# Two transformer blocks on one core: the modulation moved to TensorE's column groups, and the work around the norms reordered

## The chip, the cores and the metric

The kernel runs on one core of a Trainium2 chip. The time is that of one execution on the device in microseconds. The core's engines run in parallel and wait for each other by semaphores: TensorE (PE; its weight loads are shown apart as PEld), VectorE (DVE), ScalarE (ACT), GpSimd (POOL) and SyncE (SP). Transfers are issued from SP's and POOL's queues and carried out by 16 DMA engines.

## The reference

256 tokens of width 1024 pass through two blocks. In the first, a hybrid mixer (an mLSTM and a sliding-window attention), a cross-attention to 256 memory rows and a convolutional feed-forward net are each followed by a layer norm of the residual sum. The second block is modulated by a vector c:

```python
mod = jax.nn.silu(c) @ mod_w + mod_b            # (1, 1024) @ (1024, 6144)
shift1, scale1, gate1, shift2, scale2, gate2 = jnp.split(mod, 6)
h = rms_norm(x, g_pre_mix) * (1 + scale1) + shift1
# three branches of h (short convolution, stick-breaking attention, state space), merged with sigmoid gates
x = x + gate1 * rms_norm(merged @ w_o, g_post_mix)
h2 = rms_norm(x, g_pre_ffn) * (1 + scale2) + shift2
gt, up = jnp.split(h2 @ w_ffn_in, 2)
x = x + gate2 * rms_norm((silu(gt) * up) @ w_ffn_out, g_post_ffn)
```

All data are float32. The modulation is one vector times a matrix of 24 MB; its six vectors of 1024 are needed on all token rows.

## The kernel before

**Products.** Every float32 weight tile of 128 x 1024 is fetched into a staging tile (`wst`, four of them, from SP's queue), then split into a high and a low part of type float32r: ScalarE writes the high part (line 194), VectorE the rest (line 195). Each product is then three matmuls. Two orders are used: `mmB` (lines 369 to 373) keeps a weight tile of 128 x 128 stationary and streams 256 tokens, so that the result stands feature-major; `mmA` (lines 379 to 381) keeps 128 tokens stationary and streams up to 512 weight columns, so that it stands token-major. `weight_order` lists all weights in the order of use; `pump` splits as many of them ahead as there are homes (`WSP` = 5 pairs of tiles and, between certain points, three more by `widen`), and `done` gives a home back.

**Order of the work.** The instruction order of each engine is written out by hand: side chains are Python generators that `beside` advances by one step between matmuls, and the table `LAG` says after how many steps each goes on. `finish` ends a projection: for its last `lead` weights it does all products of token tile 0, then all of tile 1, and calls `after(tt)` as each tile's sum is complete. `boundary` builds that `after` for the four norms that stand in the way (`ln1`, `ln2`, `ln3`, and `x4`, the two norms between the mixer and the feed-forward net of the second block). It issues the norm chain of tile 0 (`layer_norm`, or `rms`, small operations on VectorE and ScalarE), then that of tile 1 interleaved with a `fill`, work for TensorE that doesn't need both tiles. `tsplit` transposes a tile's rows back to feature-major on TensorE (line 466) and splits them (lines 469 and 472).

**The feed-forward nets.** 5632 up-columns go in 11 groups `j` of 512 (256 of the gate and 256 of the value). Group 0 is done token-major by `up_first`: tile 0's part is a fill of the boundary, its result is transposed back by `turn`. The others are feature-major. The down products of earlier groups are interleaved; the last six down weights are left to `finish`.

**The modulation.** Twelve halves of 512 columns, each summed over 8 k-tiles of 128. Four halves are `raw_product`s (line 320): silu(c) of a k-tile, broadcast to 128 columns, is the stationary operand, so that the sum stands on all partitions; they are fills of the boundaries `ln2` (1), `ln3` (2) and `x4` (1), and their tiles come through the weight staging. The other eight are summed on VectorE (lines 1362 and 1364) from tiles of their own (`raw`, two buffers, SP's queue), and one matmul by ones (line 1372) brings the sum to all partitions. These steps are spread over both feed-forward nets and the branches (`mods_beside`). `mod_rows` adds the bias and multiplies the gain, which are broadcast to all partitions by transfers of 512 KB.

## Time and profile before

| | |
|---|---|
| time, median of 3 runs | 871.06 us (868.68 to 872.78) |
| the profiled execution's own time | 875.15 us |
| its span, first to last instruction | 873.4 us |
| mean granted TensorE clock | 0.987 |
| HBM read | 174.59 MB, 201 GB/s over the span |

The rows further down are of that one execution. "Busy" is the time in which an engine works on an instruction. A matmul's end is modelled, so a matmul's mean time is longer than the step to the next one; where a price per matmul is wanted, it is read from the starts. Behind "<-" stands what ended an idle time. An instruction is named by engine, line of the kernel, operation and tiles (out<-in). Float32 matmuls that are not split are issued as two instructions each.

### The profile page before, as it was taken

How to read it: one execution, taken by the hardware profiler on the slowest of the kernel's cores; microseconds unless marked ns; L12 is line 12 of the kernel's file. 1: busy time of each engine (PE TensorE's matmuls, PEld its weight loads, DVE VectorE, ACT ScalarE, POOL GpSimd, SP SyncE). 2: the span in 40 equal slices, each digit the busy share in tenths (PEclk: the TensorE clock that was granted, in tenths of full speed). 3: DMA queues.
4: the chain of work that ended last, by engine and by line, in shares of the span. 5: the costliest groups of instructions: out<-in, count | busy, mean ns of one | idle time of the engine just before them, and what ended most of it. 6: DMA issues, size and time to landing. Idle time of an engine off the chain costs nothing.

```text
span 873.4 us, 14226 instructions
## 1 busy us (share of the span) xinstructions
PE 846.1 (97%) x5580; PEld 759.5 (87%) x5580; DVE 626.6 (72%) x1047; ACT 426.2 (49%) x629; POOL 35.5 (4%) x52
## 2 busy tenths in 40 slices
PE   7999999899999999999989999999999999999996
PEld 6999878898799999999748987999995899999994
DVE  5688797665669987786777888589779765555443
ACT  5554663465256655554245645344454554444431
POOL 2000100000000000000010000002310000000000
PEclk9999999999999999999999997899999999999998
DMA  8854755285387886676186775476775686665511
GB/s 284 285 156 132 253 193 194 87 289 163 97 284 243 264 262 210 201 254 229 39 301 247 260 235 177 129 232 200 228 241 178 220 259 194 197 190 192 181 62 49
DMA packets 49860, 176.61 MB, mean 202 GB/s; under 512 B 5660, under 2 KB 5808, under 8 KB 49664
## 3 DMA queue, kind: packets, MB, share of 16 engines
q1 hardware_dynamic: 46224, 162.76, 56.9%
q0 software_dynamic: 3568, 12.92, 4.5%
q8 instruction: 44, 0.72, 0.3%
q14 instruction: 24, 0.20, 0.1%
HBM read 174.59 MB, written 1.07 MB: 201 GB/s over the span
## 4 chain that ended last, share of the span: by engine, by line
PE 74%; DMA 4%; DVE 3%; ACT 2%; issue 1%; DVEq 0%; ACTq 0%
PE pb L369 14%; PE pb L373 13%; PE pb L371 13%; PE pa L379 8%; PE pa L380 8%; PE pa L381 8%; PE pb L320 3%; DVE wl L195 2%; ACT wh L194 1%; DMA wst<-in_w_a 1%; PE pb L1372 1%; DMA wst<-in_mod_w 1%; PE pb L1172 1%; DMA wst<-in_ffn_up 1%; DMA wst<-in_xa_wq 1%
## 5 line engine op out<-in xcount | busy, mean ns | idle before, releaser
L195 DVE TENSOR_TENSOR wl<-wst,wh 128x1024 fp32r<-128x1024 f32 (+3 forms) x260 | 315.7, 1223 | 157.4 <-ACT wh L194 155.2
L194 ACT CAST wh<-wst 128x1024 fp32r<-128x1024 f32 (+3 forms) x260 | 267.5, 1036 | 274.9 <-PE pb L373 135.1
L379 PE MATMUL pa<-wh,hh 128*128 128x512 f32 x176 | 69.6, 395 | 0.0
L380 PE MATMUL pa<-wl,hh 128*128 128x512 f32 x176 | 69.2, 393 | 0.0
L381 PE MATMUL pa<-wh,hl 128*128 128x512 f32 x176 | 69.0, 392 | 0.0
L369 PE MATMUL pb<-x3h,wh 128*128 128x256 f32 x320 | 53.4, 289 | 0.0
L369 PE MATMUL pb<-x2h,wh 128*128 128x256 f32 x320 | 52.5, 286 | 0.5 <-DVE cv L626 0.5
L369 PE MATMUL pb<-x4h,wh 128*128 128x256 f32 x320 | 51.6, 283 | 0.0
L373 PE MATMUL pb<-x3l,wh 128*128 128x256 f32 x320 | 51.4, 283 | 0.0
L371 PE MATMUL pb<-x3h,wl 128*128 128x256 f32 x320 | 51.4, 283 | 0.0
L373 PE MATMUL pb<-x2l,wh 128*128 128x256 f32 x320 | 51.2, 282 | 0.0
L371 PE MATMUL pb<-x2h,wl 128*128 128x256 f32 x320 | 51.2, 282 | 0.0
L371 PE MATMUL pb<-x4h,wl 128*128 128x256 f32 x320 | 51.1, 282 | 0.0
L373 PE MATMUL pb<-x4l,wh 128*128 128x256 f32 x320 | 51.1, 282 | 0.0
L369 PEld LDWEIGHTS pb<-x2h,wh 128*128 128x128 f32 x320 | 44.4, 190 | 2.6 <-issue 1.9
L626 DVE SCALAR_TENSOR_TENSOR cv<-pb,sm,cv 128x255 f32<-128x255 f32 (+2 forms) x106 | 43.5, 473 | 3.5 <-ACT cv L622 3.5
L369 PEld LDWEIGHTS pb<-x3h,wh 128*128 128x128 f32 x320 | 44.2, 191 | 1.9 <-issue 1.6
L369 PEld LDWEIGHTS pb<-x4h,wh 128*128 128x128 f32 x320 | 44.3, 190 | 1.1 <-issue 0.5
L373 PEld LDWEIGHTS pb<-x3l,wh 128*128 128x128 f32 x320 | 44.1, 192 | 0.0
L371 PEld LDWEIGHTS pb<-x3h,wl 128*128 128x128 f32 x320 | 44.1, 191 | 0.0
L373 PEld LDWEIGHTS pb<-x2l,wh 128*128 128x128 f32 x320 | 43.9, 191 | 0.0
L371 PEld LDWEIGHTS pb<-x2h,wl 128*128 128x128 f32 x320 | 43.8, 190 | 0.0
(432 smaller groups left out, 1614.9 us busy)
## 6 DMA issues: line engine op xcount, KB each, us to landing
wst<-in_ffn_up SPq DMA_DIRECT2D x44, 512.0 KB, 4.6
wst<-in_ffn_in SPq DMA_DIRECT2D x44, 512.0 KB, 4.0
raw<-in_mod_w SPq DMA_DIRECT2D x32, 512.0 KB, 4.5
wst<-in_w_gl SPq DMA_DIRECT2D x24, 512.0 KB, 4.2
wst<-in_ffn_down SPq DMA_DIRECT2D x22, 512.0 KB, 4.2
wst<-in_ffn_out SPq DMA_DIRECT2D x22, 512.0 KB, 3.6
wst<-in_mod_w SPq DMA_DIRECT2D x16, 512.0 KB, 4.3
wst<-in_w_qk SPq DMA_DIRECT2D x12, 512.0 KB, 4.7
```

The source lines that it names most:

```text
L194: A.copy(xh, src)
L195: V.tensor_tensor(xl, src, xh.bitcast(F32), ALU.subtract)
L320: T.matmul(pm_, cs[:, k:k + 1].to_broadcast([P, P]), st[:, e, :], start=(k == 0), stop=(k == KT - 1))
L369: T.matmul(dst, wh[:, k - k0, c0:c0 + P], xh[:, k, t0:t1], start=(k == ks[0]), stop=False)
L371: T.matmul(dst, wl[:, k - k0, c0:c0 + P], xh[:, k, t0:t1], start=False, stop=False)
L373: T.matmul(dst, wh[:, k - k0, c0:c0 + P], xl[:, k, t0:t1], start=False, stop=(k == ks[-1]))
L379: T.matmul(dst[:, c0:c1], xh[:, k, tsl], wh[:, kw, c0:c1], start=first, stop=False)
L380: T.matmul(dst[:, c0:c1], xh[:, k, tsl], wl[:, kw, c0:c1], start=False, stop=False)
L381: T.matmul(dst[:, c0:c1], xl[:, k, tsl], wh[:, kw, c0:c1], start=False, stop=last)
L626: V.scalar_tensor_tensor(dst[:, j:S], ps[:, 0:S - j], taps[K - 1 - j], dst[:, j:S], ALU.mult, ALU.add)
L1172: T.matmul(pl[:, e * S:(e + 1) * S], vx[:, mt, ct * P:(ct + 1) * P], pT[:, mt, :], start=(mt == 0), stop=(mt == 1))
L1372: T.matmul(pm_, ones, acc_, start=True, stop=True)
```

## The change

- **Modulation.** All six vectors go through TensorE. For each k-tile four matmuls, each with 32 broadcast columns as the stationary operand and 256 of the 1024 columns streaming, write partitions 0 to 31, 32 to 63, 64 to 95 and 96 to 127 of one bank. Bursts of four k-tiles (12 in all) are placed in both feed-forward nets (5 and 2), in the boundary `ln3` (1) and beside the branches (4). Bias and gain are added in that layout (128 x 256, rows repeated by the host); the result goes through a small DRAM tile to all partitions. The matrix tiles of 512 KB (48) come on POOL's queue into four buffers. `raw_product`, the sums on VectorE and the matmuls by ones go.
- **Feed-forward nets.** The first two groups (`NF` = 2) are token-major. Within a k-tile pair the three kinds of matmul are grouped. Both groups of tile 0 are the fill of `ln2` and `x4`, both of tile 1 follow before the net begins.
- **Boundaries.** With `n0` = 99 tile 0's chain is issued whole; after tile 1's last product come tile 0's transposes, then the fill with a few steps of tile 1's chain before each fill step (`n4`) and `p1` splits after it; all but the last `f2` fill steps, then tile 1's transposes. `lead` is 8 for w_o (was 4), 6 for xa_wo (was 4). `ahead` allows a few splits as `finish` frees homes.
- **Homes.** `WSP` is 6; `lend` and `widen` hand out further pairs: four from the cross-attention's space for the up-columns of `ln2`, two from the tile that later holds the branches' outputs, two before `x4`. `done` splits at most two at a time.
- **Rows and tables.** Gains and biases of the norms are loaded in halves into tiles `cv0` and `cv1`, earlier than before. The attention's bias band comes ready from the host and is loaded on SP's queue, where two small matmuls, a copy and a bounce through DRAM stood. The scan's row sums are loaded by pairs of heads into two buffers instead of all at once.

The diff, cut to its core:

```diff
             for i in range(m):
+                if tt == 0:
+                    pre(items[i][2])
                 for c0, c1 in halves(ncol):
                     mmA(acc[tt], items[i][0](), 0, items[i][1], items[i][2], tt, c0, c1, first and i == 0, False)
                 if tt == 1:
                     done(go=False)
+                    freed()
                 mid()
             for c0, c1 in halves(ncol):
                 for i in range(m, n):
                     w, x, kx = items[i]
+                    if tt == 0 and c0 == 0:
+                        pre(kx)
                     mmA(acc[tt], w(), 0, x, kx, tt, c0, c1, first and i == 0, i == n - 1)
                     if tt == 1 and c1 == ncol:
                         done(go=False)
+                        freed()
                 mid()
             after(tt)
...
-    def boundary(name, chain, src, x, fill, n_fill):
+    def boundary(name, chain, src, x, fill, n_fill, before=lambda: None):
         cs_ = []
 
         def after(tt):
+            if tt == 0:
+                before()
             c = chain(tt)
             cs_.append(c)
             if tt == 0:
@@ -487,6 +480,7 @@
             c0 = cs_[0]
             while next(c0, "end") != "end":
                 drain(c, LAG[name + ".n3"])
+            pump(LAG[name + ".p0"])
             drain(fill, LAG[name + ".f0"])
             t = tsplit(src(0), x, 0)
             drain(c, LAG[name + ".n1"])
@@ -496,16 +490,26 @@
             for _ in range(n_fill - LAG[name + ".f0"] - LAG[name + ".f2"]):
                 drain(c, LAG[name + ".n4"])
                 next(fill, None)
-            n = 0
-            while next(c, "end") != "end":
-                n += 1
-                if n == LAG[name + ".p"]:
-                    pump(LAG[name + ".pn"])
+                pump(LAG[name + ".p1"])
+            drain(c)
             t = tsplit(src(1), x, 1)
             next(t)
             drain(fill)
             drain(t)
+            pump(LAG[name + ".p2"])
         return after
...
+    def ahead(name):
+        left = [LAG[name + ".t0"], LAG[name + ".t1"]]
+
+        def freed():
+            if left[0]:
+                left[0] -= 1
+            elif left[1]:
+                left[1] -= 1
+                pump(1)
+        return freed
...
     def bias():
-        pv = bankB()
-        T.matmul(pv[0:8, 0:384], rel, oh, start=True, stop=False)
-        T.matmul(pv[0:8, 0:384], ones[0:1, 0:8], mrow, start=False, stop=True)
-        band = tp.tile([8, 384], F32, tag="t", bufs=4, name="band")
-        V.tensor_copy(band, pv[0:8, 0:384])
-        d1 = dp.tile([8, 384], F32, name="d1")
-        G.dma_start(d1, band)
-        G.dma_start(kbias, bass.AP(tensor=d1.tensor, offset=d1.offset + 1, ap=[[1, P], [384, 8], [1, S]]))
+        band = a["band"]
+        nc.sync.dma_start(kbias, bass.AP(tensor=band.tensor, offset=band.offset + 1, ap=[[1, P], [384, 8], [1, S]]))
         flags.add("bias")
...
     rows = []
     wout = projA(acc, "w_out", xm, boundary("ln1", lambda tt: layer_norm(acc[tt], xs, x1, rows, tt), lambda tt: x1[:, tt, :],
-                                            xb, fill_xk(), 2 * len(fill1())), ks=(4, 5, 6, 7, 0, 1, 2, 3))
-    for k0 in (4, 6):
-        until(f"xm{k0}")
-        drain(wout, 2)
-    settle()
+                                            xb, fill_xk(), 2 * len(fill1()), before=settle), ks=(4, 5, 6, 7, 0, 1, 2, 3),
+                 lead=LAG["w_out.lead"], freed=ahead("ln1"), pre=lambda k: until(f"xm{k // 2 * 2}"))
+    until("xm4", "qk0", "qk1", "qk2", "qk3")
+    rows.extend([RowOf("ln1_g", "cv0"), RowOf("ln1_b", "cv1")])
+    drain(wout, 8 - LAG["w_out.lead"])
+    drain(wout)
...
+    def up_first(name, x, out):
+        ws, got, late_ = [], {}, []
+
+        def take(f, tt, pt):
+            got[f, tt] = tp.tile([P, 512], F32, tag="t", name=nm("up"), bufs=4)
+            out(got[f, tt], pt)
 
         def product(tt):
-            pt = bankA()
-            got.append(pt)
-            for i in range(4):
-                if tt == 0:
-                    ws.append(weights(name, i))
-                for kw in range(2):
-                    mmA(pt, ws[i], kw, x, 2 * i + kw, tt, 0, 512, i + kw == 0, i + kw == 4)
-                if tt == 1:
-                    done(go=False)
-                yield
+            while late_:
+                take(*late_.pop(0))
+            tsl = slice(tt * P, tt * P + P)
+            for f in range(NF):
+                pt = bankA()
+                for i in range(4):
+                    if tt == 0:
+                        ws.append(weights(name, 4 * f + i))
+                    (wh, wl), (xh, xl) = ws[4 * f + i], x
+                    for n, (x_, w_) in enumerate(((xh, wh), (xh, wl), (xl, wh))):
+                        for kw in range(2):
+                            T.matmul(pt, x_[:, 2 * i + kw, tsl], w_[:, kw, :], start=(i + n + kw == 0), stop=(i + n + kw == 6))
+                    if tt == 1:
+                        done(go=False)
+                    if i == 3 and tt == 0:
+                        late_.append((f, tt, pt))
+                    elif i == 3:
+                        take(f, tt, pt)
+                    yield
 
         return product, got
...
+    up1 = up_first("ffn_up0", xb, lambda st, pt: A.copy(st, pt))
+
+
+    def room2():
+        settle()
+        s_xp.close()
+        s_k8.close()
+        wider.append(widen(4, first_of["ffn_up0"] + 4 * NF, side=None))
+        pump()
...
     wo = projA(acc, "xa_wo", xo, boundary("ln2", lambda tt: layer_norm(acc[tt], x1, x2, rows, tt), lambda tt: x2[:, tt, :],
-                                          xb, raw0, 4 * len(RAW["ln2"]) - LAG["ln2.raw"] + 4), lead=LAG["wo.lead"])
-    for n in range((8 - LAG["wo.lead"]) // 2):
-        until(f"xo{n}")
-        drain(wo, 2)
-    drain(raw0, LAG["ln2.raw"])
-    settle()
+                                          xb, up1[0](0), 4 * NF, before=room2), lead=LAG["wo.lead"],
+               pre=lambda k: until(f"xo{k // 2}"), freed=ahead("ln2"))
+    until("xo0")
     drain(wo)
...
+    def act1_first(j, up0, hid, later):
         ps = [bankB(), bankB()]
-        turn(st[0], ps, 0)
-        a0, a1 = act1(0, 0, ps[0], hid), act1(0, 1, ps[1], hid)
-        later.extend([lambda: turn(st[1], ps, 1), a0[0], lambda: (a0[1](), a1[0]()), a1[1], a1[2]])
+        turn(up0[1][j, 0], ps, 0)
+        turn(up0[1][j, 1], ps, 1)
+        a0, a1 = act1(j, 0, ps[0], hid), act1(j, 1, ps[1], hid)
+        later.extend([a0[0], lambda: (a0[1](), a1[0]()), a1[1], a1[2]])
...
-    mods, rows_of = {}, {}
-
-
-    def mod_rows(half, pm_):
-        g, cs_ = half // 2, HF[half % 2]
-        if g not in mods:
+    mods = {}
+
+
+
+    raws = {}
+    n_raw = [0]
+
+    def raw_ahead():
+        if n_raw[0] < 6 * KT:
+            g, k = divmod(n_raw[0], KT)
+            raws[g, k] = fetch(mp, "raw", 4, a["mod_w"][g, k].rearrange("p (a b) -> p a b", a=4), G)
+            n_raw[0] += 1
+
+    def mod_steps():
+        for _ in range(4):
+            raw_ahead()
+        yield
+        for g in range(6):
+            bt = mp.tile([P, 2, 256], F32, tag="brow", name=nm("brow"))
+            G.dma_start(bt, a["mod_rows"][g])
+            res = mp.tile([P, 256], F32, tag="mres", name=nm("mres"), bufs=2)
+            for k0 in range(0, KT, 4):
+                pm_ = bankB()
+                for k in range(k0, k0 + 4):
+                    st = raws.pop((g, k))
+                    for j in range(4):
+                        T.matmul(pm_[32 * j:32 * j + 32, 0:256], cs[:, k:k + 1].to_broadcast([P, 32]), st[:, 256 * j:256 * j + 256],
+                                 start=(k == k0), stop=(k == k0 + 3))
+                V.tensor_tensor(res, pm_[:, 0:256], res if k0 else bt[:, 0, :], ALU.add)
+                for _ in range(4):
+                    raw_ahead()
+                if k0 + 4 < KT:
+                    yield
+            if g in (1, 4):
+                V.scalar_tensor_tensor(res, res, 1.0, bt[:, 1, :], ALU.add, ALU.mult)
+            elif g in (2, 5):
+                V.tensor_tensor(res, res, bt[:, 1, :], ALU.mult)
...
+            d = dp.tile([4, 256], F32, name=nm("d"))
+            G.dma_start(d, res[0:P:32, :])
+            G.dma_start(mods[g], d.rearrange("a b -> (a b)").unsqueeze(0).to_broadcast([P, D]))
...
-            rows3.extend([row(mp, "ln3_g"), row(mp, "ln3_b")])
+        spread(5, 2, NJ - 1, j, point)
+        if point == 1 and j == NJ - 1:
+            rows3.extend([RowOf("ln3_g", "cv0"), RowOf("ln3_b", "cv1")])
+
+            spare.extend(hilo("spare"))
+            parts_of = [tuple(t[:, 4 * i:4 * i + 4, :].rearrange("p a b -> p (a b)") for t in spare) for i in range(2)]
+            spare.append(lend(parts_of, first_of["w2_a"] + 8))
+            pump()
...
-        for h in RAW["ln3"]:
-            yield from raw_product(h)
+        mod_step()
+        yield
...
-    chains.append(mods_beside(n_steps(LAG["h.f1"], 10)))
+    chains.append(mods_beside(4))
...
-    widen(3, len(order))
+    wider.append(widen(3, len(order)))
+    wider.append(widen(2, first_of["ffn2_in0"] + 4 * NF, side=None))
+    pump()
...
-    drain(projA(acc, "w_o", xg, boundary("x4", chain4, lambda tt: hs_[tt], xb, fill4(), 4 * len(RAW["x4"]) + 4),
-                lead=LAG["w_o.lead"]))
+    def up2_out(st, pt):
+        A.activation(st[:, 0:256], pt[:, 0:256], AF.Silu)
+        V.tensor_tensor(st[:, 0:256], st[:, 0:256], pt[:, 256:512], ALU.mult)
+
+    up2 = up_first("ffn2_in0", xb, up2_out)
+
+    drain(projA(acc, "w_o", xg, boundary("x4", chain4, lambda tt: hs_[tt], xb, up2[0](0), 4 * NF),
+                lead=LAG["w_o.lead"], freed=ahead("x4")))
+    drain(up2[0](1))
+    narrow(wider.pop())
...
-        raw_rows_out()
-        spread(n_steps(10, 12), 1, NJ - 1, j, point)
+        spread(2, 3, NJ - 2, j, point)
```

## Rows read from the trace of the kernel before

**Rows 1.** The page, parts 1 and 2: busy time by engine; granted clock in 40 slices.
```profile
PE 846.1 (97%) x5580; PEld 759.5 (87%) x5580; DVE 626.6 (72%) x1047; ACT 426.2 (49%) x629; POOL 35.5 (4%) x52
...
PEclk9999999999999999999999997899999999999998
```

**Rows 2.** Stretches: length, busy us of PE, PEld, DVE, ACT, POOL, granted clock, DMA.
```profile
300.00:320.00 20.00, 20.00 (x149) 19.04 (x148) 18.27 (x28) 11.70 (x17) 0.00 (x0) 1.00 0.82 261
432.44:461.79 29.35, 24.30 (x94) 14.32 (x92) 20.61 (x45) 11.34 (x20) 2.62 (x6) 1.00 0.81 274
534.00:550.80 16.80, 15.70 (x55) 11.03 (x54) 11.26 (x23) 6.13 (x12) 0.53 (x1) 0.59 0.47 156
665.32:681.90 16.58, 14.78 (x52) 8.49 (x50) 13.22 (x38) 4.66 (x13) 0.00 (x0) 0.90 0.43 127
```

**Rows 3.** Timeline of the stick-breaking stage: start us, us, engine, line, operation, idle before.
```profile
535.24 0.70 PE L1621 MATMUL pa<-qb,kb 64*128 64x256 f32 x2 [1.10 <-DVE lk L1614]
```

**Rows 4.** Groups of instructions on PE by form: busy us, mean ns, idle before.
```profile
L320 PE MATMUL pb<-wst,cs 128*128 128x512 f32 x64 | 30.6, 623 | 1.2 <-DMA wst<-in_mod_w 1.2
...
L1372 PE MATMUL pb<-macc,triu 128*128 128x512 f32 x16 | 9.1, 650 | 0.0
```

**Rows 5.** Timeline at the second norm, PE.
```profile
231.63 3.60 PE L320 MATMUL pb<-wst,cs 128*128 128x512 f32 x8
...
235.07 1.04 PE L466 MATMUL pb<-ident,x 128*128 128x128 f32 x8
```

**Rows 6.** Groups of instructions on DVE.
```profile
L1364 DVE SCALAR_TENSOR_TENSOR macc<-raw,cs,macc 128x512 f32<-128x512 f32 x56 | 43.0, 767 | 1.1
```

**Rows 7.** Timeline of the attention's output products, PE.
```profile
518.81 0.66 PE L1640 MATMUL pb<-att,v 128*64 128x256 f32 x4
519.30 0.40 PE L1641 MATMUL pb<-att,v 128*64 128x128 f32 x4
519.62 0.74 PE L369 MATMUL pb<-x3h,wh 128*128 128x256 f32 x4
```

**Rows 8.** The same in the window 518.80 to 518.83 us.
```profile
518.81 0.44 PE L1640 MATMUL pb<-att,v 128*64 128x256 f32 x2
```

**Rows 9.** The same, weight loads.
```profile
518.81 0.20 PEld L1640 LDWEIGHTS pb<-att,v 128*64 128x64 f32 x4
```

**Rows 10.** DMA issues: queue, count, size of each, us to landing.
```profile
raw<-in_mod_w SPq DMA_DIRECT2D x32, 512.0 KB, 4.5
```

**Rows 11.** Timeline of feature-major products, PE.
```profile
568.60 0.64 PE L369 MATMUL pb<-x3h,wh 128*128 128x256 f32 x4
569.08 0.64 PE L371 MATMUL pb<-x3h,wl 128*128 128x256 f32 x4
```

**Rows 12.** Timeline of token-major products, PE.
```profile
230.47 0.40 PE L380 MATMUL pa<-wl,xoh 128*128 128x512 f32 x1
...
230.70 0.40 PE L381 MATMUL pa<-wh,xol 128*128 128x512 f32 x1
```

**Rows 13.** Timeline after the first norm, PE.
```profile
169.27 0.74 PE L369 MATMUL pa<-x1h,wh 128*128 128x256 f32 x4 [1.83 <-ACT wh L194]
```

**Rows 14.** Timeline at the second norm, tile 1's chain on DVE, first and last rows.
```profile
231.98 0.68 DVE L561 SCALAR_TENSOR_TENSOR r<-x,pa 128x512 f32<-128x512 f32 x1
...
236.99 1.41 DVE L577 SCALAR_TENSOR_TENSOR x<-x,rr,ln_b 128x512 f32<-128x512 f32 x2
```

**Rows 15.** Timeline at the third norm, tile 1's chain on DVE, first and last rows.
```profile
434.44 0.68 DVE L561 SCALAR_TENSOR_TENSOR r<-x,pa 128x512 f32<-128x512 f32 x1
...
445.77 1.42 DVE L1407 SCALAR_TENSOR_TENSOR h__760_4655<-h__760_4655,rr,mod 128x512 f32<-128x512 f32 x2
```

**Rows 16.** Timeline at the second block's boundary: tile 0's chain, and PE after it.
```profile
658.92 0.59 ACT L587 ACTIVATE junk<-pa 128x512 f32<-128x512 f32 x1
...
668.07 1.41 DVE L1407 SCALAR_TENSOR_TENSOR h__1127_7018<-h__1127_7018,rr,mod 128x512 f32<-128x512 f32 x2
668.96 1.29 PE L466 MATMUL pb<-ident,h__1127_7018 128*128 128x128 f32 x8 [1.76 <-DVE h__1127_7018 L1407]
```

## What I expect, before any run of the change

> **What bounds the kernel now.** I read the page first. TensorE is busy for 97% of the span, VectorE for 72%, and the granted clock is full in nearly every slice [rows 1]. The busy time of two mid-kernel stretches says the same: from 300 to 320 us TensorE is busy for 20.00 of 20.00 us while VectorE is busy for 18.27 [rows 2]. So in the feed-forward nets VectorE is loaded but not waited for, and work taken from it there buys nothing by itself. Work taken from TensorE counts one for one.
>
> Then I looked for time that TensorE loses, stretch by stretch [rows 2]. The hand-over to the last norm of the first block (432 to 462 us) has 24.30 busy of 29.35 us, the hand-over inside the second block (665 to 682) 14.78 of 16.58 at a granted clock of 0.90, and the stick-breaking stage (534 to 551) a granted clock of 0.59, its lower level of 1.2 GHz for most of the stretch. There the clock fell after TensorE had idled 1.10 us for VectorE amid short fp32 products [rows 3]. These places and the start and tail are the only losses worth naming, so the change can win in two ways: fewer TensorE microseconds in the modulation, or shorter waits in these stretches.
>
> **The modulation.** Before, 4 of its 12 halves are products of 8 matmuls with a broadcast stationary operand, each issued as two instructions: 64 instructions of 512 columns. The other 8 are summed on VectorE and end in one matmul by ones, 16 instructions [rows 4]. Eight of them take 235.07 - 231.63 = 3.44 us, or 0.43 each [rows 5]. TensorE spends 80 x 0.43 = 34.4 us. All of that goes, and with it 56 multiply-adds of 767 ns and 8 multiplies on VectorE [rows 6].
>
> What comes: 6 x 8 x 4 = 192 matmuls of 256 columns with 32 stationary columns, 384 instructions. By the 0.43 us per 512 columns each costs 0.215 us alone. The question is whether four column groups run at once. The trace has no such case with four, but one with two: the attention output writes partitions 0 to 63 and 64 to 127 of one bank in turn. Four instructions of 256 columns (two passes in each of two groups) take 519.30 - 518.81 = 0.49 us, where one after another would be 0.86 [rows 7]. Within the first 0.02 us both groups have started [rows 8]. So two run side by side. From line 1640's first start to the next full-width product it is 519.62 - 518.81 = 0.81 us, of which 2 x 0.215 + 2 x 0.107 = 0.64 are passes; some 0.2 us goes to changing over. Hence a burst of 4 k-tiles is 8 x 0.215 + 0.2 = 1.92 us if four groups overlap, and 12 bursts are 23.0 us. The bounds: overlap only in twos, 12 x (16 x 0.215 + 0.2) = 43.7 us; none at all, 12 x (32 x 0.215 + 0.2) = 85.0 us. I take the full overlap, since the nearest row shows each further group for nothing. Modulation: **-11.4 us** (+9.3 and +50.6 at the bounds).
>
> The four weight loads of line 1640 lie within 0.20 us, at a time when its first matmuls (0.44 us) are still running, on the same rows [rows 8, 9]. The Trainium skill, "TensorE: Matmul & The Clock Gate", section "Part 3: Packing small matmuls — row/col tiling", says that a weight load overlaps a running matmul only when its row group differs. All column groups here share all rows, so by it each of the 96 passes would show its four loads, at 0.20 us for four [rows 9] some 19 us more, and the gain would be gone. This trace disagrees, so the sum doesn't use it.
>
> **Moved transfers.** The 48 loads of the modulation (512 KB; the 32 in their own buffers land 4.5 us after issue) [rows 10] go from SP's queue to POOL's, four buffers instead of two. On SP they waited for VectorE's sums in front of the weights; on POOL they wait for a burst that TensorE has just been given. Behind them on POOL stand the small bounce, the broadcast rows, the scan's row loads and the additions into the merged tile. I cost this at nothing: POOL is busy for 35.5 us of the span [rows 1], so its queue has room, and the first five bursts spread over much of the 195 us between the second and third norm [rows 14, 15]. In the mix stage, where bursts lie closer, 2 MB per step and 0.5 MB per weight can compete; the staged and split weights cover that, and if they don't it is part of the stall case below.
>
> **Token-major columns.** One more block of 512 up-columns in each net changes from 96 matmuls of 256 columns (0.48 / 4 = 0.12 us each, 11.5 us) [rows 11] to 48 of 512 (0.23 each, 11.0 us) [rows 12]: -1.0 us for two nets. It adds 12 transposes of 1.04 / 8 = 0.13 us [rows 5], +1.6. Sum **+0.6 us**; its worth is that it fills a boundary.
>
> **Norm boundaries.** Each now runs tile 0's chain in one piece under tile 1's products, then tile 0's transposes, then a fill that needs only tile 0, while tile 1's chain runs.
> - First norm: TensorE waited 1.83 us for weight splits after the fill [rows 13]; one split per fill step now comes under it. A layer-norm chain lasts 231.98 to 236.99 + 1.41, 6.4 us [rows 14], against 5.6 us of tile-1 products (24 x 0.23), so some 0.8 us shows instead. -1.0 us.
> - Second norm: the raw product hid everything. Now the first copy shows between transposes and products, +0.5 us; the 8 token-major steps (48 x 0.23 = 11.0 us) cover the 6.4 us chain.
> - Third norm: tile 1's chain with the modulation took 434.44 to 445.77 + 1.42 = 12.75 us [rows 15]. The stretch of 29.35 us holds 28 raw instructions (12.0 us), so without a change in waiting it would become 29.35 - 12.0 + one burst of 1.9 = 19.3 us. I expect tile 0's chain 2.3 us late, 12.75 for tile 1, 1.3 to its first product, 16.4 us; up to four weight splits of 1.22 lie between, 21.3 us. The middle is no change: 0 (-3 to +2).
> - Second block: 8 instead of 4 of the w_o weights now come per token tile, so tile 1's products cover the chain of 658.92 to 668.07 + 1.41 = 10.6 us, and the wait of 1.76 us goes [rows 16]. But three of the eight weights of the fill are not yet split and queue behind tile 1's chain on VectorE. 0 (-2 to +2).
>
> **Stick-breaking stage.** VectorE loses half of the multiply-adds here, so the idle 1.10 us may go [rows 3], and with it the clock's fall, which costs 16.8 x 0.41 = 6.9 us [rows 2]. I take -2.0, between 0 and -8. The bias table from the host saves two small products in the start, which waits for loads there: 0 (to -1).
>
> **Sum.** -11.4 + 0.6 - 1.0 + 0.5 + 0 + 0 - 2.0 + 0 = -13.3 us. The profiled execution took 875.15 us, of which 873.4 are the span, so it would become 861.9. It lies 4.1 us over the median of the runs; on the median, 871.06 - 13.3 = 857.8. **Forecast 858 us.**
>
> **Rivals.**
> - *Slower: the groups overlap only in twos.* One mechanism, in the bursts: 43.7 instead of 23.0 us gives 858 + 20.7 = 879 us. It decides from an overlap of about 2.2, where 12 x (32 x 0.215 / 2.2 + 0.2) is near the 34.4 that go. For it: no row has more than two. Against: the second group cost nothing. The written order speaks for something like it too: each group's two passes are written one after the other, so if starts keep the written order, each group trails by a pass, 48 x 4 x 0.215 = 41.3 us, 876 us; but in [rows 7] the second group's line 1640 runs before the first group's line 1641, against the written order. The Trainium skill, same page and section, states that matmuls start and end strictly in order; the trace disagrees unless the build reorders, which it can't show. Chance of either 0.13.
> - *Boundary stalls.* The fills are shorter without raw products; if TensorE idles 4 us at the third norm or in the second block, the clock may fall as in [rows 2], 6.9 us for one such fall, or late weights cost as much: 865, 872 for two. For it: the 1.76 us wait was followed by a clock of 0.90. Against: the first norm's 1.83 us was not [rows 1]. Chance 0.15.
> - *The stick stage keeps its clock.* 6 us more than I took: 852. Chance 0.12.
> - My forecast, 858 (851 to 864 with the bounds of the small terms): 0.60.
>
> **Range and chances.** Something like 0.5% is what these runs can tell from no change, 866.7 to 875.4. Faster: 0.60 + 0.12 + half the stalls, 0.78. Slower: most of the first rival, 0.12. Same: 0.10. The range is 847 to 870, which leaves out the first rival and part of the double stall.
>
> **What would show it.** Right: the bursts start four matmuls within some 0.05 us and last near 1.9 us; no multiply-adds on raw tiles; TensorE's waits in the four hand-overs add to no more than now; full clock after the third norm. Wrong: bursts of 3.6 us or more, the clock at half after a hand-over, TensorE waiting for weight splits in the second block, or for loads in the mix stage.

## The result, and the profile after

| | median of runs | ratio to the kernel before | 95% interval |
|---|---|---|---|
| before | 870.41 us (868.68 to 872.78) | | |
| changed | 883.12 us (878.94 to 884.25) | 1.010 | 1.0056 to 1.0145 |
| forecast | 858 us (847 to 870) | | |

The quotient of the two medians is 1.015, at the upper end of the interval. So the change made the kernel some 1% slower (0.6 to 1.5%); I had given that 0.12. The profiled execution took 883.34 us (span 881.2), where the sum said 861.9: 21 us are to be found.

They are not in the modulation. From the page of the changed kernel (engines, clock in 40 slices, then the group of the burst products):

```profile
PE 842.3 (96%) x5796; PEld 756.9 (86%) x5796; DVE 576.1 (65%) x979; ACT 425.2 (48%) x632; POOL 64.5 (7%) x112
PEclk9999999999999999999979998899999999999999
...
L1355 PE MATMUL pb<-raw,cs 128*32 128x256 f32 x384 | 23.2, 382 | 0.0
```

And the first burst in the timeline, cut to its first 0.03 us and then whole:

```profile
295.70 0.42 PE L1355 MATMUL pb<-raw,cs 128*32 128x256 f32 x4
...
295.70 1.93 PE L1355 MATMUL pb<-raw,cs 128*32 128x256 f32 x32
297.57 0.38 PE L354 MATMUL pb<-x2h,wh 128*128 128x256 f32 x1
```

Four instructions start within 0.03 us, and 32 take 297.57 - 295.70 = 1.87 us, little more than eight passes of 0.215 us: the four column groups run side by side. All 384 are busy for 23.2 us, where I had 23.0. VectorE fell from 72% [rows 1] to 65%. Yet TensorE is busy for 842.3 us, hardly less than the 846.1 of before [rows 1], and the clock has three slices below full in mid-kernel. TensorE stands idle for 38.9 us of the span, where it was 27.3. So it waits more. Windows of the changed kernel (length, TensorE busy, granted clock, DMA share, GB/s): xa_wo; from there to the first net's loop; the hand-over at the third norm; the stick-breaking stage; w_o and the hand-over in the second block:

```profile
201.71:231.20 29.49, 27.60 (x121) 1.00 0.32 108
231.20:260.29 29.09, 26.00 (x131) 1.00 0.41 139
418.64:469.36 50.72, 42.88 (x219) 0.90 0.58 195
543.78:557.43 13.65, 12.34 (x46) 0.50 0.29 84
647.33:705.06 57.73, 50.81 (x218) 0.97 0.42 133
```

The same stretches of the kernel before, without the stick-breaking stage:

```profile
204.90:231.41 26.51, 26.51 (x122) 1.00 0.34 106
231.41:251.58 20.17, 20.17 (x86) 1.00 0.67 209
413.86:470.62 56.76, 51.71 (x220) 1.00 0.53 180
643.24:689.03 45.79, 43.99 (x180) 0.96 0.58 192
```

Each of these four stretches now leaves 1.9 to 7.8 us idle, 19.7 us in all, where before it was 6.9. At the third norm the clock goes to its lower level behind the waits, which costs up to 50.72 x 0.10 = 5.1 us. The stick-breaking stage runs at 1.2 GHz for 13.65 us, no less than before [rows 2]. What TensorE waited for (us, times, longest), in the first two windows, at the third norm, and in the second block:

```profile
PE pb L354 <- DVE cv L641: 2.8, 1, 2.8
PE pa L364 <- ACT xoh L1181: 1.9, 2, 1.2
PE pa L1220 <- ACT x2h L460: 0.2, 1, 0.2
...
PE pa L366 <- DVE x3l L463: 3.5, 1, 3.5
PE pb L457 <- DVE h__742_4702 L1403: 3.4, 1, 3.4
...
PE pa L1220 <- ACT wh L194: 2.9, 2, 1.7
PE pa L1220 <- DVE wl L195: 2.7, 3, 1.4
PE pa L1220 <- DVE x4l L463: 0.9, 1, 0.9
```

Most of this, 13.3 of 18.3 us, ends on VectorE (DVE), the rest on ScalarE, at moments when TensorE has nothing else to do. The wait of 3.5 us shows it best (timeline; a bracket is the idle time before an instruction, and what ended it):

```profile
438.66 1.84 DVE L195 TENSOR_TENSOR wl<-wst,wh 128x776 fp32r<-128x776 f32 x2
440.25 0.40 PE L365 MATMUL pa<-wl,x3h 128*128 128x512 f32 x1
440.42 0.42 DVE L1357 TENSOR_TENSOR mres<-pb,mres 128x256 f32<-128x256 f32 x1
440.87 0.42 DVE L1365 TENSOR_TENSOR mres<-mres,brow 128x256 f32<-128x256 f32 x1
441.21 0.68 DVE L576 SCALAR_TENSOR_TENSOR r<-x,pa 128x512 f32<-128x512 f32 x1
443.46 0.68 DVE L463 TENSOR_TENSOR x3l<-pb,x3h 128x512 fp32r<-128x512 f32 x1
444.20 0.50 PE L366 MATMUL pa<-wh,x3l 128*128 128x512 f32 x1 [3.55 <-DVE x3l L463]
```

The low half of tile 0 (x3l) stands in VectorE's queue behind two weight splits, the modulation's own two steps and the first steps of tile 1's chain. TensorE has transposed tile 0 and started on it, and can only wait. In the kernel before, raw products of 0.43 us each [rows 5] lay in this place.

The theory to test: **a microsecond of TensorE is worth one only where TensorE is the last to be ready.** The raw products taken away stood in hand-overs, where TensorE waits for VectorE anyway; 11 of the 12 bursts stand in loops, where it does not. Rivals: the new order of the hand-overs loses by itself (rival 1), or the moved loads do (rival 2).

### The profile page after: what moved, and what is told of

Its sections match the earlier page's. It is cut to its first block, busy times and chain, and to the rows that moved or that the text cites. A ratio compares the mean times of both kernels' runs of the same rounds, so it can differ in the third digit from the quotient of the medians.

```text
span 881.2 us, 14633 instructions
## 1 busy us (share of the span) xinstructions
PE 842.3 (96%) x5796; PEld 756.9 (86%) x5796; DVE 576.1 (65%) x979; ACT 425.2 (48%) x632; POOL 64.5 (7%) x112
## 3 DMA queue, kind: packets, MB, share of 16 engines
HBM read 174.02 MB, written 1.09 MB: 199 GB/s over the span
## 4 chain that ended last, share of the span: by engine, by line
PE 73%; DVE 7%; ACT 2%; issue 2%; DMA 1%; POOL 0%; DVEq 0%; ACTq 0%
PE pb L354 13%; PE pb L356 13%; PE pb L358 13%; PE pa L364 6%; PE pa L366 6%; PE pa L365 6%; PE pa L1220 4%; PE pb L1355 2%; DVE wl L195 2%; ACT wh L194 1%; PE pa L358 1%; PE pa L356 1%; PE pa L354 1%; PE pb L1178 1%; PE pb L1152 1%
## 5 line engine op out<-in xcount | busy, mean ns | idle before, releaser
L201 POOL DMA_DIRECT2D raw<-in_mod_w x48 | 25.2, 530 | 389.4 <-PE pb L1355 301.3
L354 PE MATMUL pb<-x2h,wh 128*128 128x256 f32 x288 | 47.2, 287 | 2.8 <-DVE cv L641 2.8
L356 PE MATMUL pb<-x2h,wl 128*128 128x256 f32 x288 | 46.5, 284 | 0.0
L358 PE MATMUL pb<-x2l,wh 128*128 128x256 f32 x288 | 46.3, 283 | 0.0
L354 PE MATMUL pb<-x4h,wh 128*128 128x256 f32 x288 | 46.2, 283 | 0.0
L358 PE MATMUL pb<-x4l,wh 128*128 128x256 f32 x288 | 46.0, 282 | 0.0
L356 PE MATMUL pb<-x4h,wl 128*128 128x256 f32 x288 | 46.0, 282 | 0.0
L354 PEld LDWEIGHTS pb<-x2h,wh 128*128 128x128 f32 x288 | 40.2, 193 | 5.5 <-issue 4.3
L354 PEld LDWEIGHTS pb<-x4h,wh 128*128 128x128 f32 x288 | 39.8, 190 | 1.3 <-issue 0.4
L356 PEld LDWEIGHTS pb<-x2h,wl 128*128 128x128 f32 x288 | 39.9, 193 | 0.0
```

The lines of the kernel that those rows point to most:

```text
L201: (queue or nc.sync).dma_start(st[:, :n].rearrange("p (a b) -> p a b", a=src.shape[1]), src)
L354: T.matmul(dst, wh[:, k - k0, c0:c0 + P], xh[:, k, t0:t1], start=(k == ks[0]), stop=False)
L356: T.matmul(dst, wl[:, k - k0, c0:c0 + P], xh[:, k, t0:t1], start=False, stop=False)
L358: T.matmul(dst, wh[:, k - k0, c0:c0 + P], xl[:, k, t0:t1], start=False, stop=(k == ks[-1]))
```

## The experiments

For the comparisons below the span is cut into stages by TensorE's own products: the first one that reads xo, the last of xa_wo, the last up-product of the first net, the first unit of the mix, the first of w_o, and the last of all. Lengths in us, one profiled execution each:

| kernel | start, first norm | xa_wo | second norm, first net | third norm | mix | second block, second net | tail | span |
|---|---|---|---|---|---|---|---|---|
| before | 204.9 | 26.5 | 182.5 | 56.8 | 172.6 | 221.7 | 8.5 | 873.4 |
| before, no modulation | 205.1 | 26.5 | 181.9 | 50.8 | 167.3 | 221.0 | 8.4 | 861.1 |
| before with bursts | 210.2 | 26.5 | 192.2 | 52.9 | 175.5 | 223.0 | 8.4 | 888.7 |
| changed | 201.7 | 29.5 | 187.4 | 50.7 | 178.0 | 225.5 | 8.4 | 881.2 |
| changed, no modulation | 203.1 | 29.5 | 177.2 | 49.3 | 167.4 | 220.9 | 8.4 | 855.8 |
| four vectors on VectorE, mended | 200.4 | 27.7 | 179.8 | 48.1 | 172.8 | 221.0 | 8.7 | 858.6 |

The first stage differs by 5 us between profiles of kernels whose start is the same (205 and 210 in those made from before), so the other stages tell more than the span. The mix has a spread of its own: how long the lower clock lasts in its stick-breaking stage differs from trace to trace, from nothing to 17.07 us, and up to half of that time is lost.

**1 and 2. Both kernels without modulation.** The loads, products and sums go, the rows are the biases. In the kernel before, the empty steps stay in the hand-overs.

```diff
-            use(("raw", 4 * half + i), product)
-            raw_used.add(("raw", 4 * half + i))
             yield
-        raw_rows.append((half, pm_))
+        raw_rows.append((half, None))
...
-        V.tensor_tensor(res[:, cs_], pm_, mb[:, cs_], ALU.add)
+        V.tensor_copy(res[:, cs_], mb[:, cs_])
```

> The kernel before with the modulation's loads, products and sums left out (the modulation rows are the bias rows alone). 34.4 us of TensorE work go. Theory (lost cover): the 28 raw products at the three hand-overs were what hid the norm chains, so the hand-overs open and the time falls by only about 17 us, to 853, with the clock at half after the third norm or in the second block. Rival 1 (the new order of the hand-overs loses by itself): nothing opens here, the time falls by nearly all of it, to about 837. Rival 2 (transfers): the 24 MB of loads count too, 837 or less.

Measured: 866.35 us, ratio 0.9932 (0.9898 to 0.9966). 34.4 us of TensorE work left, and the time fell by 0.7%, about 6 us: less than even the theory expected. Windows of the second norm, third norm and second block, and the waits in them:

```profile
231.56:253.62 22.06, 16.56 (x70) 0.85 0.18 62
413.47:464.28 50.81, 41.37 (x188) 0.87 0.39 129
631.61:677.53 45.92, 38.76 (x164) 0.93 0.45 151
```

```profile
PE pa L370 <- ACT x2h L460: 2.8, 1, 2.8
PE pa L372 <- DVE x2l L463: 2.7, 1, 2.7
...
PE pa L370 <- ACT x3h L460: 3.1, 2, 2.9
PE pa L371 <- DVE wl L195: 3.0, 1, 3.0
...
PE pb L457 <- DVE h__1068_6830 L1387: 4.1, 1, 4.1
```

The hand-overs open: where the raw product hid the second norm, 5.5 us are idle (0 before) and the clock falls; at the third norm 9.4 us are idle (5.1 before); in the second block 7.2 (1.8 before). The first window shows how the saving is lost. The raw product of 6.9 us is gone from it, and it is 1.9 us longer than before: 5.5 us of idle time and 22.06 x 0.15 = 3.3 us by the lower clock make up the 8.8. By stages, 9.5 us of products left the first net's stage and 0.6 came off it; 13.8 left the third norm's and 5.9 came off; 7.7 left the second block's and 0.7 came off.

In the changed kernel:

```diff
-            raws[g, k] = fetch(mp, "raw", 4, a["mod_w"][g, k].rearrange("p (a b) -> p a b", a=4), G)
...
-                V.tensor_tensor(res, pm_[:, 0:256], res if k0 else bt[:, 0, :], ALU.add)
+                if k0 == 0:
+                    V.tensor_copy(res, bt[:, 0, :])
```

> The changed kernel with the modulation's loads and products left out (rows are the bias rows alone). 23 us of bursts go. Theory: the bursts cost what they last and little of it was cover, so about 862, within some 8 us of the kernel before without its modulation. Rival 1: the same 862, but 15 us or more above the kernel before without its modulation. Rival 2 (the loads on POOL's queue delay the weights): the loads' harm goes too, 852 or less.

Measured: 859.69 us, ratio 0.9851 (0.9818 to 0.9885), against 1.010 with the bursts: 2.5%, some 22 us. The bursts, 23.2 us, show in full: 10.3 us in the first net (5 bursts, 9.6 us), 10.6 in the mix (4, 7.7 us), 4.6 in the second net (2, 3.8 us). And without modulation the new order is the faster one, by 0.8%: rival 1 is false.

**3. Raw halves packed, in the same places.** A half's sum then stands in four groups of 32 partitions, so it goes through ScalarE and a small DRAM tile to all partitions; the rest is as before.

```diff
-                    T.matmul(pm_, cs[:, k:k + 1].to_broadcast([P, P]), st[:, e, :], start=(k == 0), stop=(k == KT - 1))
+                    for j in range(4):
+                        T.matmul(pm_[32 * j:32 * j + 32, 0:128], cs[:, k:k + 1].to_broadcast([P, 32]), st[:, e, 128 * j:128 * j + 128],
+                                 start=(k == 0), stop=(k == KT - 1))
```

> The kernel before, with only its four raw halves packed in four column groups of 128 columns: 27.5 us of products become 6.9, in the same places; VectorE's eight halves, order, queues and hand-overs stay. Theory: the time falls by far less than the 20.6 us saved, by 4 to 12 (859 to 867), because the chains at the hand-overs now show, with a clock at half behind one or two of them. Rival 1 (the new order is the cause): nearly all of it is gained, about 851. Rival 2 (transfers): as rival 1, since the loads stay on SP's queue.

Measured: 873.33 us beside 873.61 for before, ratio 1.0011 (0.998 to 1.0042). Nothing. Against 30.6 us of busy time [rows 4] the packed products have

```profile
L321 PE MATMUL pb<-wst,cs 128*32 128x128 f32 x256 | 9.1, 276 | 2.4 <-DMA wst<-in_mod_w 2.4
```

so 21.5 us left TensorE in the same places, and all of it came back, as waiting and as a lower clock (0.85 at the second norm, 0.91 at the third). At the third norm the waits are for weight splits, 6.1 us on ScalarE's half and 3.3 on VectorE's; at the second norm and in the second block they are for the norm's chain. The theory had expected a gain of 4 to 12 us.

**4. One token-major group.**

```diff
-NF = 2
+NF = 1
```

> The changed kernel with one token-major group per net in place of two. Theory: the stall at the start of the first net (some 3 us and half clock behind it) goes, but the fill at the second norm and in the second block is 5.6 us in place of 11, under the 6.4 and 10.6 us of their chains: 878 to 886, the gain at one place given back at the other. Rival (the second group is the main cause): 873 or less.

Measured: 881.97 us, ratio 1.0112 (1.0072 to 1.0152): as with two. The wait of 2.8 us for the convolution (line 641) at the start of the first net goes, and in its place one for the second norm comes (2.7 us for tile 1's rows, line 592), which the shorter fill no longer covers. It's a trade.

**5. The lead in xa_wo.**

```diff
-    "wo.lead": 6
+    "wo.lead": 4
```

> The changed kernel, with 4 instead of 6 of the xa_wo weights at the end of that product (the lead of before). The stage from xa_wo's first product to its last took 26.5 us before and 29.5 in the changed kernel, with and without modulation. Theory: the lead of 6 makes TensorE wait for the last two attention heads, so the 3.0 us come back there, 880. Rival: the wait is owed to the earlier start after the first norm (3.2 us gained there) and stays wherever the lead ends, 883.

Measured: 880.22 us, ratio 1.0086 (1.0053 to 1.0119); the stage took 27.74 us. So 1.75 of the 3.0 us were the lead. Of the other 1.2, 0.7 are a wait for xo that remains; the rest stays open. The gain in the whole time is within the noise.

**6. Bursts without their loads.**

```diff
-            raws[g, k] = fetch(mp, "raw", 4, a["mod_w"][g, k].rearrange("p (a b) -> p a b", a=4), G)
+            if n_raw[0] < 4:
+                kept.append(fetch(mp, "raw", 4, a["mod_w"][g, k].rearrange("p (a b) -> p a b", a=4), G))
+            raws[g, k] = kept[n_raw[0] % 4]
```

> The changed kernel with all 192 burst matmuls, but only the first 4 of the modulation's 48 loads; every burst works on these four tiles. Theory (the bursts cost their own length, the loads nothing): 881 to 884, as with the loads. Rival (22 MB on POOL's queue hold back the weights and stretch the mix stage, where four bursts cost 10.1 us instead of 7.7): 878 or less, the mix stage down by 2 us or more.

Measured: 882.13 us, ratio 1.01 (1.0065 to 1.0135), the mix no shorter than with the loads (179.4 us against 178.0). HBM reads fell from 174.02 to 150.95 MB for nothing: rival 2 is false.

**7. Three bursts moved into the hand-overs.**

```diff
-        spread(5, 2, NJ - 1, j, point)
+        spread(4, 2, NJ - 1, j, point)
...
+    def fill4():
+        mod_step(hold=True)
+        yield
+        for i, _ in enumerate(up2[0](0)):
+            if i == 3:
+                mod_step(hold=True)
+            yield
```

> The changed kernel with three of its 12 bursts moved into waits: two in the hand-over at the third norm in place of one, and the last two in the second block's hand-over in place of the second net; VectorE reads the burst's bank a step later. Theory (TensorE time is free in these hand-overs and costs its length elsewhere): 3 x 1.92 = 5.8 us less, and up to two falls of the clock of 1.7 us each avoided, 874 to 878. Rival (a burst in a hand-over delays the chain behind it or waits for its loads): no change, 881 to 885.

Measured: 876.94 us, ratio 1.0035 (1.001 to 1.006). From 1.010 that is 0.65%, 5.7 us, where 3 x 1.92 = 5.8 were expected from the place alone. Windows of the third norm and the second block in this kernel:

```profile
416.79:464.79 48.00, 42.62 (x252) 0.96 0.72 250
644.22:702.98 58.76, 54.08 (x283) 0.97 0.50 167
```

At the third norm there is a burst more and the stage is 2.7 us shorter: 5.4 us idle instead of 7.8, and up to 48.00 x 0.04 = 1.9 us by the clock instead of 5.1. In the second block two bursts, 3.8 us, cost 1.0. Since VectorE also reads a burst's bank later here, which takes two steps out of x3l's way (its wait is 2.8 us), this run doesn't tell place and order apart at the third norm.

**8. The chains shortened.** At the third norm and in the second block the modulated norm is left out.

```diff
-            yield from modulated(x3, 0, tt)
+            hs_[tt] = x3[:, tt, :]
```

> The changed kernel with the modulated norm left out of the chains at the third norm and in the second block (the norm's or the sum's rows go straight to the transposes); bursts, weights, loads and fills stay. Theory (the length of VectorE's chains sets the waits there, now that no product covers them): the hand-overs at the third norm (50.7 us between its anchors) and in the second block (57.7) shorten by 4 to 8 us each and keep the full clock, 868 to 874. Rival (late weight splits or loads set these waits): both stay within 2 us, 880 to 884.

Measured: 869.73 us, ratio 0.9948 (0.9926 to 0.9969). The same two windows, and the longest wait in the first:

```profile
418.60:459.98 41.38, 38.61 (x219) 1.00 0.70 237
639.40:691.71 52.31, 49.55 (x219) 0.97 0.44 148
...
PE pa L366 <- DVE x3l L463: 1.9, 1, 1.9
```

9.3 and 5.4 us less, with the same 219 and 218 products as the changed kernel (one more counted in the second), and the full clock at the third norm, which is up to 5.1 of the 9.3 us. So the length of VectorE's chain sets most of the waiting here. In the second block the clock is at 0.97 as in the changed kernel, and a wait of 1.7 us for a late weight split remains, so splits have a part there.

**9. Four of the six vectors summed on VectorE**, their sum over partitions as one product of four column groups, the other two as bursts inside the hand-overs.

```diff
+            if g not in (2, 5):
+                acc_ = mods[g] = mp.tile([P, D], F32, tag=f"mod{g % 3}", name=nm("mod"))
+                for k in range(KT):
...
+                        V.scalar_tensor_tensor(acc_, st, cs[:, k:k + 1], acc_, ALU.mult, ALU.add)
...
+                pm_ = bankB()
+                for j in range(4):
+                    T.matmul(pm_[32 * j:32 * j + 32, 0:256], ones[:, 0:32], acc_[:, 256 * j:256 * j + 256], start=True, stop=True)
```

> As the kernel with three bursts moved, but four of the six modulation vectors are summed on VectorE (32 multiply-adds of 1024 columns, about 1.4 us each) and only their sum over partitions is a TensorE product, in four column groups: 4 x 0.63 = 2.5 us in place of 8 bursts of 1.92 = 15.4; the two other vectors are bursts inside the two hand-overs. Theory (VectorE has room in the nets and the mix stage, TensorE has none outside the hand-overs): the changed kernel without modulation, 859.7, plus 2.5 and some 2 to 4 us for the hand-overs, 863 to 867, so faster than before by about 1%. Rival (VectorE is the next bound: its 45 us delay the conversions and the splits): 873 or more.

Measured: 877.22 us, ratio 1.0035 (1.0 to 1.007). A miss: the mix came down to 75.5 us (up to the last stick product) from 85.1, but the first net's loop rose from 158.4 to 164.4. (Not all of the mix's gain is VectorE's: the lower clock lasts 6.83 us there, and 13.65 in the changed kernel.) The waits in the first net:

```profile
PE pb L1382 <- DVE mod L1377: 10.8, 2, 6.6
```

Twice TensorE stood at the product over partitions for the last multiply-add of its vector. That is order, not VectorE's load.

**10. The same, mended:** two empty steps ahead of that product (with the counts of steps that go with them), and the lead of 4 in xa_wo.

```diff
                     raw_ahead()
                     yield
+                yield
+                yield
                 pm_ = bankB()
```

> As the kernel that sums four of the six vectors on VectorE, with two empty steps between a vector's last multiply-add and the product that sums it over partitions, and a lead of 4 in xa_wo. Theory (TensorE waited 10.8 us for the last multiply-add, twice, and lost more by the clock behind each wait): these waits go, 16 us less in the first net's loop, some 2 in xa_wo, 859 to 863. Rival (VectorE is full in the first net and the wait moves to the conversions): 868 or more.

Measured: 858.64 us beside 873.63 for before, ratio **0.9827** (0.9809 to 0.9845). Faster than both kernels, 1.7% under before. Engines, third norm and second block:

```profile
PE 827.3 (96%) x5572; PEld 748.2 (87%) x5572; DVE 607.0 (71%) x1007; ACT 424.1 (49%) x632; POOL 63.7 (7%) x112
...
408.01:456.11 48.10, 43.46 (x251) 0.93 0.71 246
628.92:686.24 57.32, 52.48 (x283) 1.00 0.51 172
```

VectorE is at 71%, about where it was before the change [rows 1]; TensorE's modulation is down to

```profile
L1393 PE MATMUL pb<-raw,cs 128*32 128x256 f32 x128 | 8.1, 383 | 2.1 <-DMA raw<-in_mod_w 2.1
L1384 PE MATMUL pb<-mod,triu 128*32 128x256 f32 x32 | 3.0, 452 | 0.0
```

of which the 8.1 lie in hand-overs. The first net's loop is 150.3 us, 2.2 over the changed kernel without modulation. (That kernel's 859.69 us are no lower bound for this one, since it has the lead of 6.)

**11. The first two vectors as bursts again.**

```diff
-            if g not in (2, 5):
+            if g in (3, 4):
```

> As that kernel, but with the first two vectors as bursts in the first net, so that VectorE sums only two, in the mix stage: 8 bursts of 1.92 us, 4 of them in hand-overs. Theory: the first net's loop as with bursts (156.4), the mix stage as with VectorE's sums (75.5), 863 to 867; 4 to 6 us over the kernel with four vectors on VectorE. Rival (what was saved in the mix stage was chance): 872 or more.

Measured: 861.35 us, ratio 0.987 (0.9848 to 0.9892), under the expected 863 to 867, and 0.4% (some 4 us) over the last one: four bursts of 7.7 us against two vectors on VectorE. The stages show more than the sum. The second norm and first net take 186.6 us instead of 179.8, nearly the bursts' whole length; the mix takes 165.1 instead of 172.8, and that is the clock. Here is the mix of this run, then the stretch at the lower clock in the mix of run 10:

```profile
465.00:630.08 165.08, 163.24 (x1325) 1.00 0.69 223
...
520.37:537.44 17.07, 16.77 (x63) 0.50 0.42 130
```

So by these two profiles the bursts cost more than the 4 us, and the clock gave some of it back.

**12. The modulation part of the change alone**, in the kernel before.

```diff
-        for n, q in enumerate(parts):
...
-                    V.scalar_tensor_tensor(acc_, st[:, e, :], cs[:, k:k + 1], acc_, ALU.mult, ALU.add)
+        for g in range(6):
...
+                    for j in range(4):
+                        T.matmul(pm_[32 * j:32 * j + 32, 0:256], cs[:, k:k + 1].to_broadcast([P, 32]), st[:, 256 * j:256 * j + 256],
+                                 start=(k == k0), stop=(k == k0 + 3))
```

> The modulation part of the change alone: the kernel before, its hand-overs, leads and token-major column left as they are, with the 12 column-group bursts, the loads on POOL's queue and the rows from the host of the changed kernel in place of raw products and VectorE's sums (the scan's rows go through smaller buffers, as in the changed kernel, to make room). By its TensorE work it should gain 11.4 us. Theory (the raw products stood where TensorE waits anyway, the bursts stand where it doesn't): the kernel before without modulation, 866, plus about 23, 886 to 892. Rival (the reordered hand-overs and the second token-major group are what lost): 860 to 866.

Measured: 887.30 us, ratio 1.0157 (1.0112 to 1.0202). The part that was to gain 11.4 us loses 1.6%, some 14, and over the same kernel without modulation it is 2.25% or 20 us. The rest of the change wins back about 0.6%, which the intervals don't separate from nothing; without modulation it was 0.8%, and there they do.

## Why the prediction was wrong

By stages, the forecast's terms against the two profiled executions (us):

| stage | forecast, and its terms | measured |
|---|---|---|
| start, first norm | -1.0 | -3.2 |
| xa_wo | 0 | +3.0 |
| second norm, first net | +0.9 (-9.5 products, +9.6 bursts, +0.3 token-major, +0.5 norm) | +5.0 |
| third norm | -11.9 (-13.8 products, +1.9 burst, 0 waits) | -6.0 |
| mix | +2.3 (-3.4 sums, +7.7 bursts, -2.0 stick) | +5.3 |
| second block, second net | -3.6 (-7.7 products and sum, +3.8 bursts, +0.3 token-major, 0 waits) | +3.8 |
| sum | -13.3 | +7.8 (with the tail's -0.1) |

- **Overlap of four groups: right**, 23.2 us for the bursts against 23.0. The rivals of twos (43.7 us) and of a group trailing by a pass (41.3 us) are false. (The overlap at which the bursts equal the 34.4 us is 2.6, not 2.2: at 2.2 the sum given there is 39.9 us.) By the rule on weight loads of the Trainium skill, "TensorE: Matmul & The Clock Gate", section "Part 3: Packing small matmuls — row/col tiling", some 19 us more would have shown, by the prediction's estimate; the trace disagrees here too, since a burst is no longer than its passes and the changing over.
- **"Work taken from TensorE counts one for one": the step that failed.** I read it from the first net's loop [rows 2] and applied it to all 34.4 us, 27.5 of which stood in hand-overs. Without any modulation the kernel before is only 6 us faster (12.4 between the two profiles), so some 22 to 28 of the 34.4 bought nothing: they came back as idle time and as a lower clock. What the change gave up was worth 6, what it put in cost 20 to 22. The Trainium skill, "Perfetto Trace Analysis", section "Identifying the Most-Contended Engine", tells one to optimize the engine with the highest occupancy first, TensorE here (97%, and 87% by its weight loads [rows 1]). The runs bear that out for the loops, where the bursts cost their length, and not for the hand-overs. The next section there, "Optimization Strategy", says that a kernel can have regimes in which the most-contended engine changes; the hand-overs, where TensorE waits for VectorE, are such regimes here.
- **The terms that should have held this were the hand-overs', and they were mis-sized.** I did say that the raw product hid the second norm; then I priced what it hid at +0.5, 0 (-3 to +2) and 0 (-2 to +2). Measured against the table's products the three stages came out 4.1, 5.9 and 7.4 us worse. At the second norm the token-major groups did cover the chain (TensorE waited 0.2 us for x2h). The loss is behind them: a wait of 2.8 us for VectorE's convolution at the start of the first net, which was no term of the sum, and then a stretch at the lower clock, which costs half its length:

```profile
260.47:263.89 3.42, 3.42 (x18) 0.50 0.29 114
```

For the third norm I allowed for splits between tile 0's chain and the products, not for the modulation's own steps and the start of tile 1's chain, which stand in VectorE's queue too: 2.8 us more idle than before, and up to 5.1 us by the clock, which was in no term of the sum. In the second block I named the late splits and allowed 2 us; the waits for them are 5.6 us.
- **xa_wo** was not in the sum: +3.0, of which 1.75 us are the lead of 6.
- **The rival of boundary stalls** had the mechanism and the clock, at 865 to 872 and a chance of 0.15. It counted two places, there were four, and it took the raw products' whole length as gained beside them.
- **First norm**: better than forecast, by 2.2 us, in a stage that differs by 5 us between kernels with the same start. **Token-major columns**: no difference that can be measured, as the +0.6 said. **Moved loads at nothing**: right, shown by the bursts without them.
- **Stick-breaking stage**: the -2.0 did not come. VectorE has less to do there, but TensorE's wait of 1.1 us is still there, and the half clock lasts 13.65 us as before.
- **The mix** is 3 us over its forecast, 2.0 of it this term. Its four bursts seem to cost 10.6 us rather than 7.7, and that is the clock too. The mix of the changed kernel, then of the same without modulation, and the stretch at the lower clock in the latter:

```profile
469.36:647.33 177.97, 175.56 (x1437) 0.96 0.62 202
...
459.05:626.44 167.39, 164.97 (x1309) 0.98 0.53 164
529.08:535.91 6.83, 6.83 (x31) 0.50 0.15 46
```

13.65 us at half clock instead of 6.83 cost some 3 us; the other 7 to 8 are the bursts.

## What to carry to other kernels

Before you count a microsecond taken from the busiest engine, ask where it stands: work that lies in a hand-over, between a chain on another engine and what waits for it, is filler, and taking it out moves little until the chain gets shorter. The cheap test is to leave the whole piece of work out and time that; here it would have said, before any rewriting, that in this order of the work the modulation could give at most 0.7%. And put what remains of the work into those same hand-overs, or on the engine that has room all along, with enough steps between a sum and the product that reads it.

## What the runs showed of the hardware

- Four column groups of 32 run side by side: 32 instructions of 256 columns take 1.87 us, where eight passes of 0.215 would be 1.72. Packed in instructions of 128 columns, four halves take 9.1 us (256 instructions), where 6.9 would follow from the column count. They stand in several pieces, and each piece pays for the changing over: 16 instructions that stand alone take 0.65 us, where four passes of 0.107 would be 0.43.
- A multiply-add of 1024 columns on VectorE takes less than two of 512: 1279 ns against 2 x 767 [rows 6], from this group of the mended kernel:

```profile
L1377 DVE SCALAR_TENSOR_TENSOR mod<-raw,cs,mod 128x1024 f32<-128x1024 f32 x28 | 35.8, 1279 | 0.1
```

- The clock fell to its lower level at the waits in the hand-overs: granted 0.85 to 0.93 over three stages of the kernel before without modulation, whose longest single waits are 2.8 to 4.1 us. With the shortened chain, whose longest wait at the third norm was 1.9 us, it stayed at 1.00 there; but in its second block, with no wait over 1.7 us, it was 0.97. The same wait does not always end the same way: in the stick-breaking stage of runs 10 and 11 TensorE waits 1.1 us for VectorE (tile lk, line 1653); behind it the clock is at its lower level for 17.07 us in run 10, and stays full in run 11.
- 23 MB of loads more or less, on a queue of their own, could not be seen in the time.
